# Column sums of squares in a hybrid decoder step: from one float32 product with ones to two float32r products of a larger and a smaller part

## The chip, the cores and the metric

The kernel runs on one core of a Trainium2 chip. The metric is the device time of one execution in microseconds (us); the figure of a kernel is the median of its runs. One execution is also recorded by the hardware profiler, and that record (the page and the trace) is what is read here.

## The reference, cut to what matters

The kernel computes one step of a two-layer decoder for 1024 prompt tokens and 64 sample tokens (1088 columns in all). What the change touches are the sums of squares over the feature axis in three kinds of normalisation:

```
def rmsnorm(x, g):                      # x: (tokens, 1024), before each mixer, each MLP and at the end
    y = xf * rsqrt(mean(xf * xf, axis=-1) + EPS)
    return y * g

def l2norm(x):                          # q and k of each of 4 DeltaNet heads, 128 features
    return xf * rsqrt(sum(xf * xf, axis=-1) + EPS)

o = rmsnorm(o, g_norm) * silu(gate)     # output of each of 8 HGRN2 heads, 128 features
```

Everything else (the projections, the delta rule, latent attention over pages, the HGRN2 recurrence, two squared-ReLU MLPs) is unchanged.

## The kernel before

Activations lie with features on the 128 partitions and tokens along the free axis, in three chunks of 384, 384 and 320 columns. A sum over features is therefore a sum over partitions, and the kernel takes it on TensorE: a product of the squares with a 128 by 128 block of ones leaves the sum in every partition of a PSUM bank.

Dense layers use float32r operands. Each float32 operand is split into a larger part (a ScalarE copy to float32r, line 265) and a smaller part (the float32 value minus that copy, on VectorE, line 266), and three products are added (lines 335 to 337, and 1661 to 1663 for the MLP's second half). The products with ones, on the other hand, have plain float32 operands; the trace shows each as two MATMUL records.

The stages, in time: phase A (0 to about 1040 us: the input projection with its convolution and head work, paged attention of the sample group, prompt attention, the delta rule, the output projection), MLP 0 (to about 1810), the HGRN2 layer (to about 2500), MLP 1 (to about 3262) and the end of the final norm. The three places that the change touches:

- **Norms of x** (`squares`, `split_x`, `inv_rms`, `final_norm`). For each chunk ScalarE squares the eight feature blocks, GpSimd adds blocks 0 to 6 into `ssa` (line 286), the eighth square stays apart in `ssl`, and two float32 products (line 295) add both in one bank. Logarithm, exponential and a Newton step follow (lines 296 to 304) and give `rb`, by which every later evacuation of the projection is multiplied. Four of these norms go through `split_x`; the last, `final_norm`, writes the output at line 1698.
- **Heads of the DeltaNet** (`pairs`). For each of 4 heads, six pieces (k and q, three chunks each): a square (line 699), one float32 product (line 695), logarithm and exponential (689, 690) and a multiplication (691). Behind them stand three blocks of decays: a broadcast load into tile `he` (line 712), sums into `hd` (716), exponentials (717, 718), products of keys (728), and stores to `U_d` and `A_d` (733). `he` and `hd` have one buffer each.
- **Heads of HGRN2** (`core`). For each of 8 heads the squares of the output are gathered in `o2` (line 1883); at the head's end three float32 products (line 1935), logarithms, an exponential, a multiplication and a store. The levels at the head's start write their inputs to tiles of tag `y` (two buffers; lines 1814, 1815, 1818, 1819), which the products at line 1797 read.

Work is written as generators that are woven by weights (`weave`), and a scheduler then orders the instructions of each engine by its own simulated timeline, so each edit can move instructions far from it. Within an engine the order is then fixed. `core(h)` is woven two to one with `proj(h + 1)`, the projection of the next head, whose dense products fill TensorE between the steps of the head.

Of the kernel before, what the change touches and what calls it, by code (L numbers as in the profile page):

```python
# [19 lines left out]
NT = 1088  # L20
# [151 lines left out]
def setup(k, nc, tc, A, O, ctx):  # L172
    k.nc, k.tc, k.A, k.O, k.ctx = nc, tc, A, O, ctx
    k.P = lambda name, bufs=1, **kw: tc.tile_pool(name=name, bufs=bufs, **({} if kw.get("space") == DRAM else {"reuse_waits": "tile"}), **kw)
    k.cp = ctx.enter_context(k.P("consts"))
    k.cst = k.cp.tile([128, NCST], F32, name="cst")
    k.vec = k.cp.tile([128, NVEC], F32, name="vec")
    k.eps = k.cp.tile([128, 2], F32, name="eps")
    k.rb = k.cp.tile([128, NT], F32, name="rb")
    k.dr = ctx.enter_context(k.P("dr", space=DRAM))  # L180
    nc.scalar.preload_act_table_set(EXP_SET)
    nc.gpsimd.memset(k.eps[:, 0:1], EPS)
    nc.gpsimd.memset(k.eps[:, 1:2], EPS * 128)
    C = lambda o, n, p=128: k.cst[0:p, o:o + n]
    k.ident, k.tri, k.maskT = C(C_ID, 128), C(C_TRI, 128), C(C_MT, 128)
    k.tri8, k.mk8, k.ones, k.ones8 = C(C_TRI8, 64, 64), C(C_MK8, 64, 64), C(C_ONE, 128), C(C_ONE8, 64, 64)
    k.V = lambda o: k.vec[:, o:o + 1]
# [76 lines left out]
def split_pair(k, hi, lo, src, eng=None):  # L264
    k.nc.scalar.copy(hi, src)  # L265
    (eng or k.nc.vector).tensor_tensor(lo, src, hi.bitcast(F32), ALU.subtract)  # L266


def rsqrt_from(k, out, ps, scale, bias):

    nc = k.nc
    nc.scalar.activation(out, ps, AF.Ln, bias=bias, scale=scale)
    nc.scalar.activation(out, out, AF.Exp, scale=-0.5)


def squares(k, pool, x, c, n):

    nc = k.nc
    T = lambda tag, name: pool.tile([128, 384], F32, tag=tag, bufs=2, name=name)[:, :n]
    acc = t = T("ssa", f"ssa{c}")  # L280
    for kk in range(8):
        if kk:
            t = T("ssq", f"ssq{c}{kk}") if kk < 7 else T("ssl", f"ssl{c}")
        nc.scalar.activation(t, x[:, kk], AF.Square)  # L284
        if 0 < kk < 7:
            nc.gpsimd.tensor_tensor(acc, acc, t, ALU.add)  # L286
        yield acc, t


def inv_rms(k, pool, sq, c, n, r, ps):  # L290

    nc = k.nc
    p = ps()[:, :n]
    for i in range(2):
        nc.tensor.matmul(p, k.ones, sq[i], start=i == 0, stop=i == 1)
    nc.scalar.activation(r, p, AF.Ln, bias=k.eps[:, 0:1], scale=1.0 / 1024)
    nc.scalar.activation(r, r, AF.Exp, scale=-0.5)
    yield

    v, r2 = (pool.tile([128, 384], F32, tag="nwt", bufs=2, name=f"nwt{c}{i}")[:, :n] for i in range(2))  # L300
    nc.vector.tensor_scalar(v, p, -0.5 / 1024, -0.5 * EPS, ALU.mult, ALU.add)
    nc.scalar.activation(r2, r, AF.Square)
    nc.vector.tensor_tensor(v, v, r2, ALU.mult)
    nc.vector.scalar_tensor_tensor(r, v, 1.5, r, ALU.add, ALU.mult)
    yield


def split_x(k, pool, sqp, x, c, n, g_off, r, ps, xs, lag):

    nc = k.nc  # L310
    hi = pool.tile([128, 8, n], F32R, tag=f"xh{c}", name=f"xh{c}")
    lo = pool.tile([128, 8, n], F32R, tag=f"xl{c}", name=f"xl{c}")
    xs[c] = [(hi[:, kk], lo[:, kk]) for kk in range(8)]
    yield
    s = squares(k, sqp, x, c, n)
    for kk in range(8):
        nc.scalar.mul(hi[:, kk], x[:, kk], k.V(g_off + kk))
        nc.vector.scalar_tensor_tensor(lo[:, kk], x[:, kk], k.V(g_off + kk), hi[:, kk].bitcast(F32),  # L318
                                       ALU.mult, ALU.subtract)
        sq = next(s)  # L320
        yield
    for _ in range(lag):
        yield
    yield from inv_rms(k, sqp, sq, c, n, r, ps)
# [101 lines left out]
def in_proj(k):  # L426
# [247 lines left out]
    def pairs(h, ys, z):  # L674
# [7 lines left out]
        yield  # L682
        items = [(t, t0, n) for t in (kn, q) for t0, n in CH]
        T = lambda i: rp.tile([128, 384], F32, tag="nq", bufs=3, name=f"nq{h}{i}")[:, :items[i][2]]
        r, ps = {}, {}
        for i in range(len(items) + 2):
            if i > 1:
# [4 lines left out]
            if 0 < i <= len(items):  # L692
                n = items[i - 1][2]
                ps[i - 1] = k.mm()[:, :n]
                nc.tensor.matmul(ps[i - 1], k.ones, r[i - 1], start=True, stop=True)
            if i < len(items):
                t, t0, n = items[i]
                r[i] = T(i)
                nc.scalar.activation(r[i], t[:, t0:t0 + n], AF.Square)
            yield  # L700
        nc.sync.dma_start(k.y_d[h, 1], kn)
        egl, egs = k.egl[h], k.egs[h]
# [1001 lines left out]
def hgrn(k, X, before):  # L1704
# [61 lines left out]
    def core(h):  # L1766
# [150 lines left out]
        for c in range(8):  # L1917
# [12 lines left out]
            St = Sn  # L1930
            yield 0.9
        nc.sync.dma_start(O["hgrn_p"][h], St)
        for c, (t0, n) in enumerate(CH):
            p = k.sm()
            nc.tensor.matmul(p[:, :n], k.ones, o2[:, t0:t0 + n], start=True, stop=True)  # L1935
            nc.scalar.activation(o2[:, t0:t0 + n], p[:, :n], AF.Ln, bias=epsd, scale=1.0 / 128)
        nc.scalar.activation(o2, o2, AF.Exp, scale=-0.5)
        nc.vector.tensor_tensor(oz, oz, o2, ALU.mult)
# [57 lines left out]
```

## Time and profile before

| | us |
|---|---|
| median of 3 runs (lowest, highest) | 3300.77 (3298.63, 3304.87) |
| the profiled execution's own time | 3298.84 |
| span of its record | 3297.1 |
| TensorE busy, matmul records | 3163.4 (96%) |
| VectorE / ScalarE / GpSimd busy | 1709.0 / 1107.8 / 543.8 |

Busy time of TensorE is modelled from pipelined records that overlap, so the distance from one record's start to the next is read for a price, and the idle time ahead of an instruction for a wait. A row of the timeline gives start, duration, engine, line, operation, output and inputs, shape and, in brackets, the idle time before it with what ended it; records of one kind that follow one another are merged (x2, x4).

### The profile page before, as it was taken

How to read it: one execution, taken by the hardware profiler on the slowest of the kernel's cores; microseconds unless marked ns; L12 is line 12 of the kernel's file. 1: busy time of each engine (PE TensorE's matmuls, PEld its weight loads, DVE VectorE, ACT ScalarE, POOL GpSimd, SP SyncE). 2: the span in 40 equal slices, each digit the busy share in tenths (PEclk: the TensorE clock that was granted, in tenths of full speed). 3: DMA queues.
4: the chain of work that ended last, by engine and by line, in shares of the span. 5: the costliest groups of instructions: out<-in, count | busy, mean ns of one | idle time of the engine just before them, and what ended most of it. 6: DMA issues, size and time to landing. Idle time of an engine off the chain costs nothing. (4 is left out here: it accounts for less than half of the span.)

```text
span 3297.1 us, 63998 instructions
## 1 busy us (share of the span) xinstructions
PE 3163.4 (96%) x26944; PEld 2928.9 (89%) x26944; DVE 1709.0 (52%) x3102; ACT 1107.8 (34%) x2046; POOL 543.8 (16%) x581
## 2 busy tenths in 40 slices
PE   8999998899989999999999999999899999999997
PEld 7777875687878999999999989889799999999997
DVE  5324443665537445444546555555656444444446
ACT  5334433344415221122123445544535122212212
POOL 3021224112102000000001344443522000000002
PEclk9999999999999999999999999999899999999999
DMA  4666668422132111111112111111322111111111
GB/s 147 199 224 202 218 225 288 149 74 94 57 115 84 45 45 42 43 52 46 33 52 77 56 53 54 53 58 43 131 73 64 33 52 52 45 33 52 46 39 55
DMA packets 140279, 288.70 MB, mean 88 GB/s; under 512 B 16536, under 2 KB 85496, under 8 KB 139992
## 3 DMA queue, kind: packets, MB, share of 16 engines
q1 hardware_dynamic: 118248, 210.60, 19.4%
q10 hardware_dynamic: 12528, 40.45, 3.8%
q0 software_dynamic: 9216, 33.56, 3.1%
q8 instruction: 212, 3.47, 0.4%
q14 instruction: 75, 0.61, 0.1%
HBM read 235.48 MB, written 49.08 MB: 86 GB/s over the span
## 5 line engine op out<-in xcount | busy, mean ns | idle before, releaser
L335 PE MATMUL mm<-xh,wh 128*128 128x384 f32 (+1 forms) x2808 | 936.9, 334 | 12.4 <-ACT wh L265 11.2
L337 PE MATMUL mm<-xh,wl 128*128 128x384 f32 (+1 forms) x2808 | 929.2, 331 | 0.2 <-DVE wl L266 0.2
L336 PE MATMUL mm<-xl,wh 128*128 128x384 f32 (+1 forms) x2808 | 929.0, 331 | 0.0
L1664 DVE TENSOR_TENSOR xr<-xr,sm 128x384 f32<-128x384 f32 (+1 forms) x768 | 404.8, 531 | 430.5 <-PE sm L1663 430.4
L335 PEld LDWEIGHTS mm<-xh,wh 128*128 128x128 f32 x2808 | 531.4, 189 | 23.3 <-ACT wh L265 11.2
L337 PEld LDWEIGHTS mm<-xh,wl 128*128 128x128 f32 x2808 | 531.0, 189 | 9.5 <-issue 6.5
L336 PEld LDWEIGHTS mm<-xl,wh 128*128 128x128 f32 x2808 | 531.0, 189 | 9.1 <-issue 5.1
L1661 PE MATMUL sm<-hh,dh 128*128 128x384 f32 (+1 forms) x1536 | 505.0, 329 | 6.6 <-DVE xr L1664 5.2
L1663 PE MATMUL sm<-hh,dl 128*128 128x384 f32 (+1 forms) x1536 | 503.2, 328 | 0.0
L1662 PE MATMUL sm<-hl,dh 128*128 128x384 f32 (+1 forms) x1536 | 502.5, 327 | 0.0
L286 POOL TENSOR_TENSOR ssa<-ssa,ssq 128x384 f32<-128x384 f32 (+1 forms) x90 | 95.1, 1057 | 1725.0 <-ACT ssq L284 1722.1
L1638 ACT ACTIVATE hraw<-hraw 128x384 f32<-128x384 f32 (+1 forms) x192 | 96.9, 505 | 689.7 <-DVE hraw L1637 689.6
L1661 PEld LDWEIGHTS sm<-hh,dh 128*128 128x128 f32 x1536 | 288.8, 188 | 9.9 <-DVE xr L1664 7.5
L1662 PEld LDWEIGHTS sm<-hl,dh 128*128 128x128 f32 x1536 | 288.6, 188 | 0.6 <-issue 0.2
L1663 PEld LDWEIGHTS sm<-hh,dl 128*128 128x128 f32 x1536 | 288.7, 188 | 0.0
L1637 DVE SCALAR_TENSOR_TENSOR hraw<-mm,rb 128x384 f32<-128x384 f32 (+1 forms) x192 | 102.7, 535 | 184.6 <-PE mm L337 184.5
L265 ACT CAST dh<-dr 128x1024 fp32r<-128x1024 f32 x64 | 66.9, 1048 | 389.6 <-PE sm L1662 381.2
L266 DVE TENSOR_TENSOR hl<-hraw,hh 128x384 fp32r<-128x384 f32 (+1 forms) x192 | 102.3, 533 | 114.8 <-ACT hh L265 114.8
L265 ACT CAST wh<-wr 128x1024 fp32r<-128x1024 f32 x96 | 100.7, 1049 | 137.2 <-PE mm L336 135.3
L266 DVE TENSOR_TENSOR wl<-wr,wh 128x1024 fp32r<-128x1024 f32 x96 | 122.3, 1275 | 37.3 <-ACT wh L265 37.2
L265 ACT CAST hh<-hraw 128x384 fp32r<-128x384 f32 (+1 forms) x192 | 94.9, 494 | 5.1
L928 POOL DMA_INDIRECT lt<-in_lat,ix x64 | 67.0, 1046 | 159.1 <-PE sc L885 66.0
(659 smaller groups left out, 4522.0 us busy)
## 6 DMA issues: line engine op xcount, KB each, us to landing
la<-in_latT SPq DMA_DIRECT2D x256, 144.0 KB, 4.2
wr<-in_w_up SPq DMA_DIRECT2D x64, 512.0 KB, 3.4
dr<-in_w_down ACTq DMA_DIRECT2D x64, 512.0 KB, 4.3
wr<-in_w_in_c SPq DMA_DIRECT2D x32, 512.0 KB, 3.5
win<-in_w_in_ab SPq DMA_DIRECT2D x21, 512.0 KB, 3.9
y_d<-y SPq DMA_DIRECT2D x12, 544.0 KB, 3.1
oC_d<-g SPq DMA_DIRECT2D x8, 544.0 KB, 3.8
q_d<-q SPq DMA_DIRECT2D x16, 256.0 KB, 3.4
```

Of the source, the lines that this page charges most:

```text
L265: k.nc.scalar.copy(hi, src)
L266: (eng or k.nc.vector).tensor_tensor(lo, src, hi.bitcast(F32), ALU.subtract)
L286: nc.gpsimd.tensor_tensor(acc, acc, t, ALU.add)
L335: nc.tensor.matmul(acc, wh[:, kk], xh, start=f, stop=False)
L336: nc.tensor.matmul(acc, wh[:, kk], xl, start=False, stop=False)
L337: nc.tensor.matmul(acc, wl[:, kk], xh, start=False, stop=l)
L1637: nc.vector.scalar_tensor_tensor(raw[:, s], p[:, :n], 0.0, k.rb[:, s], ALU.max, ALU.mult)
L1638: nc.scalar.activation(raw[:, s], raw[:, s], AF.Square)
L1661: nc.tensor.matmul(p[:, :n], wh[:, m], hh[:, s], start=a, stop=False)
L1662: nc.tensor.matmul(p[:, :n], wh[:, m], hl[:, s], start=False, stop=False)
L1663: nc.tensor.matmul(p[:, :n], wl[:, m], hh[:, s], start=False, stop=b)
L1664: nc.vector.tensor_tensor(k.xr[c][:, m], k.xr[c][:, m], p[:, :n], ALU.add)
```

## The change

`ones` gets a float32r copy, `onesr`, made once at the start on GpSimd. `col_sums` adds two products with it, of a larger and a smaller part. The heads' squares (six pieces in each of 4 heads; the whole `o2` in each of 8 heads) are split by `split_pair` first. In `split_x` the two partial sums of x are added on GpSimd, then split, then multiplied; `final_norm` keeps its two float32 products. The split parts of the DeltaNet pieces take the tiles `he` and `hd`; those of `o2` take both buffers of `y`.

```
+    k.onesr = k.cp.tile([128, 128], F32R, name="onesr")
+    nc.gpsimd.memset(k.rb[:, 0:128], 1.0)
+    nc.gpsimd.tensor_copy(k.onesr, k.rb[:, 0:128])
...
+def col_sums(k, p, hl):
+    for i in range(2):
+        k.nc.tensor.matmul(p, k.onesr, hl[i], start=i == 0, stop=i == 1)
...
 def squares(k, pool, x, c, n):
-            t = T("ssq", f"ssq{c}{kk}") if kk < 7 else T("ssl", f"ssl{c}")
+            t = T("ssq", f"ssq{c}{kk}")
...
 def inv_rms(k, pool, sq, c, n, r, ps):
-    for i in range(2):
-        nc.tensor.matmul(p, k.ones, sq[i], start=i == 0, stop=i == 1)
+    if sq[0] is not None:
+        for i in range(2):
+            nc.tensor.matmul(p, k.ones, sq[i], start=i == 0, stop=i == 1)
+    else:
+        col_sums(k, p, sq[1])
...
 def split_x(k, pool, sqp, x, c, n, g_off, r, ps, xs, lag):
+    nc.gpsimd.tensor_tensor(sq[0], sq[0], sq[1], ALU.add)
+    yield
+    hl = [sqp.tile([128, 384], F32R, tag="ss" + i, bufs=1, name=f"ss{i}{c}")[:, :n] for i in "hl"]
+    split_pair(k, *hl, sq[0])
+    sq = None, hl
...
     def pairs(h, ys, z):
+        TR = lambda i, j: rp.tile([128, 512], F32R, tag="hd" if j else "he", bufs=1, name=f"nh{h}{i}{j}")[:, :items[i][2]]
...
-                nc.tensor.matmul(ps[i - 1], k.ones, r[i - 1], start=True, stop=True)
+                col_sums(k, ps[i - 1], hl)
...
                 nc.scalar.activation(r[i], t[:, t0:t0 + n], AF.Square)
+                hl = TR(i, 0), TR(i, 1)
+                split_pair(k, *hl, r[i])
...
     def core(h):
+        hl2 = [hl.tile([128, NT], F32R, tag="y", bufs=2, name=f"oh{h}{i}") for i in range(2)]
+        split_pair(k, *hl2, o2)
         for c, (t0, n) in enumerate(CH):
             p = k.sm()
-            nc.tensor.matmul(p[:, :n], k.ones, o2[:, t0:t0 + n], start=True, stop=True)
+            col_sums(k, p[:, :n], [t[:, t0:t0 + n] for t in hl2])
```

Line numbers of the changed kernel are up to 21 higher: 265 becomes 268, 712 becomes 731, 733 becomes 752, 1664 becomes 1683, 1698 becomes 1717, 1818 becomes 1837, 1883 becomes 1902, 1936 becomes 1957.

What moves, at three places. First ScalarE at the end of one HGRN2 head: `o` is `o2` of the head that ends, `k`, `f`, `x` and `y` belong to the next one. Before:

```order
L1818 COPY y_22809<-k_22760 128x544
L1817 ACTIVATE x_22808<-f_21915 128x544
L1883 ACTIVATE o_22403<-os_22418 128x64
L1883 ACTIVATE o_22403<-sm 128x128
L1875 DMA S_23209<-in_shg 128x1024
```

In the changed kernel, at the same head's end:

```order
L1902 ACTIVATE o_22578<-sm 128x128
L268 CAST oh_22821<-o_22578 128x1088
L1831 COPY x_23059<-f_22090 128x272x2
L1832 ACTIVATE x_23059<-x_23059 128x1088
L1837 COPY y_22991<-k_22942 128x544
L1957 ACTIVATE o_22578<-sm,epsd 128x384 x2
L1957 ACTIVATE o_22578<-sm,epsd 128x320
```

The next head's first `y` (L1818, now L1837) stood ahead of all eight steps of the head that ends; now it stands behind the new split of `o2`.

Second SyncE's queue around the last DeltaNet head. `he<-cum_d` is the load of a decay block, `U_d` and `A_d` the stores of a block's results. The load of the first block stood some fifty rows above these rows. Before:

```order
L360 DMA cq1r<-cq_d 128x2x512
L360 DMA uq1r<-in_w_uq 128x4x256
L733 DMA U_d<-hu_6987 128x512
L733 DMA A_d<-ha_6990 128x512
L712 DMA he_7002<-cum_d 128x4x128
```

In the changed kernel:

```order
L376 DMA cq1r<-cq_d 128x2x512
L376 DMA uq1r<-in_w_uq 128x4x256
L731 DMA he_7087<-cum_d 128x4x128
L752 DMA U_d<-hu_7125 128x512
L752 DMA A_d<-ha_7128 128x512
L731 DMA he_7140<-cum_d 128x4x128
```

The first block's load has come down to stand directly ahead of that block's stores, behind the last of the head's six products.

Third VectorE in the final norm: `xr` are the residual's chunks, L1664 (now L1683) adds a product of the MLP to one, L1698 (now L1717) writes the normalised output of one. Before:

```order
L304 SCALAR_TENSOR_TENSOR rb<-nwt_34642,rb 128x384
L1664 TENSOR_TENSOR xr_26759<-xr_26759,sm 128x320
L1698 SCALAR_TENSOR_TENSOR xr_26758<-xr_26758,vec,rb 128x384 x4
L1664 TENSOR_TENSOR xr_26759<-xr_26759,sm 128x320
L1698 SCALAR_TENSOR_TENSOR xr_26758<-xr_26758,vec,rb 128x384 x4
L301 TENSOR_SCALAR nwt_34703<-sm 128x320
```

In the changed kernel:

```order
L315 SCALAR_TENSOR_TENSOR rb<-nwt_34881,rb 128x384
L1683 TENSOR_TENSOR xr_26976<-xr_26976,sm 128x320
L1717 SCALAR_TENSOR_TENSOR xr_26975<-xr_26975,vec,rb 128x384 x7
L1683 TENSOR_TENSOR xr_26976<-xr_26976,sm 128x320
L1717 SCALAR_TENSOR_TENSOR xr_26975<-xr_26975,vec,rb 128x384
L312 TENSOR_SCALAR nwt_34942<-sm 128x320
```

The last addition to the third chunk stands behind seven output rows of the second instead of four.

## Rows read from the trace of the kernel before

**Rows 1.** Page: busy time of the engines, share of the span, instructions
```profile
PE 3163.4 (96%) x26944; PEld 2928.9 (89%) x26944; DVE 1709.0 (52%) x3102; ACT 1107.8 (34%) x2046; POOL 543.8 (16%) x581
```
**Rows 2.** Windows: HGRN2 stage, end (length, busy PE PEld DVE ACT POOL, clock, DMA)
```profile
1870.00:2345.00 475.00, 452.33 (x5623) 422.31 (x5611) 272.35 (x425) 223.18 (x312) 215.47 (x164) 0.99 0.14 49
3262.00:3297.10 35.10, 18.09 (x85) 14.29 (x83) 25.55 (x46) 11.06 (x23) 11.10 (x12) 0.77 0.36 128
```
**Rows 3.** Timeline of PE: one float32 product among float32r products, 384 and 320 columns
```profile
49.87 0.81 PE L528 MATMUL mm<-cqs,cst 128*128 128x384 f32 x2
50.22 0.63 PE L335 MATMUL mm<-xh,wh 128*128 128x384 f32 x1
50.69 0.34 PE L336 MATMUL mm<-xl,wh 128*128 128x384 f32 x1
51.04 0.34 PE L335 MATMUL mm<-xh,wh 128*128 128x384 f32 x1
...
1946.27 0.70 PE L1935 MATMUL sm<-o,cst 128*128 128x320 f32 x2
1946.96 0.31 PE L335 MATMUL mm<-xh,wh 128*128 128x320 f32 x1
```
**Rows 4.** Source line 695: durations min/median/max in ns, first and last start, shapes
```profile
L695 PE MATMUL mm<-nq,cst x48: 431/485/591, 203.2 to 511.4; 128*128 128x384 f32 x32, 128*128 128x320 f32 x16
```
**Rows 5.** Page, groups: count | busy us, mean ns | idle before, releaser
```profile
L286 POOL TENSOR_TENSOR ssa<-ssa,ssq 128x384 f32<-128x384 f32 (+1 forms) x90 | 95.1, 1057 | 1725.0 <-ACT ssq L284 1722.1
L266 DVE TENSOR_TENSOR hl<-hraw,hh 128x384 fp32r<-128x384 f32 (+1 forms) x192 | 102.3, 533 | 114.8 <-ACT hh L265 114.8
L265 ACT CAST wh<-wr 128x1024 fp32r<-128x1024 f32 x96 | 100.7, 1049 | 137.2 <-PE mm L336 135.3
L266 DVE TENSOR_TENSOR wl<-wr,wh 128x1024 fp32r<-128x1024 f32 x96 | 122.3, 1275 | 37.3 <-ACT wh L265 37.2
```
**Rows 6.** Waits of PE (total, times, longest): products that wait for a split's smaller part
```profile
PE mm L336 <- DVE o2l L266: 2.2, 2, 1.8
PE mm L336 <- DVE o4l L266: 1.9, 2, 1.5
PE mm L336 <- DVE ol L266: 0.5, 1, 0.5
PE mm L336 <- DVE o0l L266: 0.4, 1, 0.4
```
**Rows 7.** Timeline of ACT, POOL and PE: the next head's first tiles, and its first products
```profile
2133.85 0.69 ACT L1818 COPY y<-k 128x544 f32<-128x544 f32 x1
2136.27 2.12 POOL L1819 TENSOR_TENSOR y<-x,q 128x544 f32<-128x544 f32 x1 [5.30 <-ACT x L1817]
2142.01 1.60 POOL L1815 TENSOR_TENSOR y<-x,q 128x544 f32<-128x544 f32 x1
...
2169.78 0.80 PE L1797 MATMUL sm<-q,k 128*32 128x32 f32 x68
```
**Rows 8.** Timeline of SP and DVE: a decay block of the last DeltaNet head
```profile
521.54 0.36 SPq L712 DMA_DIRECT2D he<-cum_d  x1
526.27 1.14 DVE L716 SCALAR_TENSOR_TENSOR hd<-he,nb,cst 128x128 f32<-128x128 f32 x4 [2.04 <-DMA he<-cum_d]
```
**Rows 9.** Timeline of DVE: output rows of the final norm
```profile
3281.53 3.00 DVE L1698 SCALAR_TENSOR_TENSOR xr<-xr,vec,rb 128x384 f32<-128x384 f32 x4
3284.85 2.19 DVE L1698 SCALAR_TENSOR_TENSOR xr<-xr,vec,rb 128x384 f32<-128x384 f32 x4
```
**Rows 10.** Timeline of PE: waits ahead of the first norm's products
```profile
20.30 0.91 PE L295 MATMUL mm<-ssa,cst 128*128 128x384 f32 x2 [1.42 <-POOL ssa L286]
32.04 0.91 PE L295 MATMUL mm<-ssa,cst 128*128 128x384 f32 x2 [1.85 <-POOL ssa L286]
```
**Rows 11.** Timeline of DVE: one multiplication while GpSimd ran subtractions, and one without
```profile
494.98 0.56 DVE L691 TENSOR_TENSOR y<-y,nq 128x384 f32<-128x384 f32 x1 [1.80 <-ACT nq L690]
495.75 4.76 DVE L691 TENSOR_TENSOR y<-y,nq 128x384 f32<-128x384 f32 x1 [0.22 <-ACT nq L690]
```

## The prediction

> **What bounds the kernel now.** The page's first section comes first: matmul records fill 96% of the span on TensorE, the next engine stands at 52% [rows 1]. Busy time of overlapping records proves little, so I look next at the windows: in the HGRN2 stage TensorE is without a record for 475 - 452.3 = 22.7 us, one twentieth [rows 2]. Time taken from TensorE there is therefore time taken from the span, as long as no new wait appears in its place. The end is another thing: in its last 35.1 us VectorE is busy for 25.6 and TensorE for 18.1 [rows 2]. There the order on VectorE decides.
>
> **What the products cost.** From the timeline of TensorE, by starts: from a float32 product of 384 columns at 49.87 to 50.69 is 0.82 us, with one float32r product in it (start 50.22); a float32r product takes (51.04 - 50.69) / 2 = 0.175 us [rows 3]. So the float32 product holds the engine for 0.645 us, two float32r products for 0.35. With 320 columns: 1946.96 - 1946.27 = 0.69, less one float32r product (0.175 x 320/384 = 0.146), is 0.544 us; two float32r products are 0.292 [rows 3].
> - DeltaNet heads: 48 records, two for each product, 32 of 384 columns and 16 of 320 [rows 4], so 16 and 8 products. Saved: 16 x 0.295 + 8 x 0.252 = 6.7 us.
> - HGRN2 heads: 8 heads with the same three chunks, so again 16 and 8 products of the same kind, 6.7 us.
> - Norms of x: four of the five change, each with chunks of 384, 384, 320. Two float32 products become two float32r products: 4 x (2 x (1.29 - 0.35) + (1.088 - 0.292)) = 10.7 us.
>
> Together **-24.1 us** on TensorE, all in stages that it fills.
>
> **What is added elsewhere.** ScalarE gets 36 copies to float32r of a chunk and 8 of 1088 columns (1.05 x 1088/1024 = 1.11 us), VectorE as many subtractions (0.53 us, and 1.275 x 1088/1024 = 1.35), GpSimd 12 additions of 1.06 [rows 5]. As engine time this is free, since those engines are busy 52%, 34% and 16% [rows 1]; if TensorE did not cover it, it would be 8 x 2.46 us for the HGRN2 heads alone. It costs by being late:
>
> *Splits before a product.* 44 new splits stand directly ahead of a product (12 norms, 24 pieces, 8 heads). The trace has 44 splits of that kind in the output projections (`ol`, `wol`, `o0l` to `o4l`), and TensorE waited 2.2 + 1.9 + 0.5 + 0.4 = 5.0 us for their smaller parts [rows 6]. The bounds are 0, if the scheduler puts enough dense products between the copy and the product, and 44 x 1.1 = 48, if every split were as exposed as the two of `o2l` (2.2 / 2). The new splits are of the size of `ol` and `wol`, 34 of those 44, of which the rows show one wait of 0.5. I take the mean over all 44: **+5.0 us**.
>
> *The last DeltaNet head.* `he` and `hd` are taken by the split pieces, so the load for the first decay block now waits for the sixth product. For the first three heads the dense products behind it cover that; for the last they are finished, and the prompt preparation's stores queue on SyncE behind the block's stores. From the load's issue to the end of the four sums is 526.27 + 1.14 - 521.54 = 5.9 us [rows 8], with exponentials some 7. Bounds 0 and +7. I take **+2**, nearer the lower: the sample group's attention, which needs nothing of this head, is still being worked off on TensorE then (by the order of the work; no row prices that cover).
>
> *HGRN2 heads.* The split of `o2` takes both `y` buffers, so the next head's first two `y` tiles wait until the column sums are read. Now they are done early: the second ends at 2142.01 + 1.60 = 2143.6, and its products follow those of 2169.78 [rows 7]. Afterwards the path between two heads has the split (1.11 + 1.35) and then y0 (2.12) and y1 (two of 1.60): 7.8 us more. The dense products of the next projection cover it if there are enough of them; the head is woven with 288, about 47 us of TensorE. I cost it at nothing beyond the splits above; without that cover it is a rival below. What is late next is the multiplication of level two on GpSimd.
>
> *Front.* TensorE waited 1.42 and 1.85 us for GpSimd's sums [rows 10]. Each now becomes an addition (1.06), a copy and a subtraction longer, but other dense products are ordered ahead. Bounds -3.3 (both waits filled) and +2.1 (one chain of 1.06 + 0.5 + 0.53 exposed); taken as 0. Making `onesr` on GpSimd, idle then, costs nothing; the first chunk's sums would feel it otherwise.
>
> *End.* `final_norm` keeps its products, but three more output rows go before the last addition: 3 x 2.19/4 = 1.6 us, or 3 x 3.00/4 = 2.3 [rows 9]. Against that the last addition of 384 columns comes ahead of the first eight output rows, which frees a bank earlier. Bounds -1 and +2.3; taken **+1**.
>
> Sum: -24.1 + 5.0 + 2 + 1 = -16.1 us. The profiled execution took 3298.84 us, which gives 3282.7; it lies 1.9 below the median of the runs, so on the scale of the median **3285 us**. A difference of 0.2%, 6.6 us, is about what a measurement can tell from none.
>
> **A rule that speaks against it.** One multiplication of 384 columns took 0.56 us alone and 4.76 while GpSimd ran subtractions [rows 11]. The Trainium skill, "SBUF — State Buffer", section "SBUF: two separate sides", says that a VectorE operation with two SBUF inputs and a GpSimd operation lock each other out of a shared port pair for a whole instruction. The added subtractions are of that kind; by that rule each would be held for up to one GpSimd operation, and the row agrees. This is rival B.
>
> **The rivals.**
> - A, everything is gained: the waits of rows 10 are filled and no split is waited for. -24.1 - 3.3 = -27 us, 3273. For it: the scheduler has put dense products between the larger and the smaller part's product. Against: rows 6. Chance 0.12.
> - B, the splits eat most of it: the subtraction is held behind a GpSimd operation of 1.06 us [rows 5] in half of the 44 splits, and half of that reaches TensorE: 22 x 1.06 x 0.5 = 11.7 more than forecast, 3297. For: row 11; in HGRN2 GpSimd is busy 215 of 475 us [rows 2]. Against: in the norms it has ended its own sums by then. Chance 0.14.
> - C, slower: the path from head to head bounds HGRN2, because `y` is not free. There are seven head boundaries with 7.8 us each. From 16.1 / 7 = 2.3 us exposed at each the gain is gone; with half of the 7.8 exposed at all seven it is 27 more than forecast, 3312. For: 22.7 us in which TensorE already stands, part of it for `y`. Against: y0 and y1 were ready 26 us early [rows 7], so the path had slack. Chance 0.10.
> - D, the change doesn't do what it says: a product of `onesr` runs at the float32 rate, so nothing is saved and 48 products of some 0.6 us come on top, 3301 + 29 + 8 = 3338. Against: weights made by the same copy run at 0.175 us [rows 3]. Chance 0.02.
>
> **How the numbers follow.** The forecast, a gain of 7 to 24 us, has 0.62. Faster by over 0.2%: 0.62 + 0.12 and 0.02 of B, 0.76. Within 0.2%: the rest of B with a little of C, 0.13. Slower: most of C and D, 0.11. The range runs from A, 3273, to C's beginning with two boundaries wholly exposed, 3285 + 15.6, 3300.
>
> **What would show it.** The records of lines 695 and 1935 gone, 120 of `col_sums` in their place at 0.175 us from start to start; line 295's down to 12 for the final norm. Waits of TensorE for `nh`, `ssl` or `oh` near 5 us in total. In HGRN2 a window shorter by about 6 us for the same dense work; if it is not shorter, and products with `y` wait on GpSimd after each boundary, C is right. Between 511 and 560 us the first use of the next stage at most 2 us late. At the end the last addition about 1 us later against the start of the final norm. The prediction is wrong if the waits on TensorE grow by more than 17 us, or by none.

## The result, and the profile after

| | before | after |
|---|---|---|
| median (lowest, highest), us | 3302.07 (3298.63, 3305.09) | 3335.39 (3324.58, 3341.0) |
| ratio of after to before, 95% interval | | 1.0102, 1.0084 to 1.012 |
| the profiled execution's own time, its span | 3298.84, 3297.1 | 3330.14, 3328.4 |

The change is 33 us slower where 16 us faster was forecast; the time lies 35 us above the range. The page of the changed kernel gives the busy times that answer to [rows 1]:

```profile
PE 3157.2 (95%) x26920; PEld 2940.0 (88%) x26920; DVE 1769.9 (53%) x3146; ACT 1139.3 (34%) x2096; POOL 557.1 (17%) x595
```

TensorE has 6 us less to do than before, VectorE 61 us more. Where the time went is seen by stage. From the first evacuation of HGRN2's first projection (line 1762, now 1781) to the last head's last multiplication (1938, now 1959) it was 626.9 us and is 669.2. The windows of that stage, before (columns as in [rows 2]):

```profile
1820.90:2447.80 626.90, 590.41 (x6859) 548.56 (x6858) 353.12 (x554) 287.62 (x405) 259.43 (x191) 0.97 0.18 60
```

After, and below it one period of the seventh head, from the first GpSimd tile of one head to that of the next:

```profile
1816.00:2485.20 669.20, 606.76 (x6929) 572.38 (x6928) 387.85 (x565) 304.72 (x421) 257.13 (x191) 0.94 0.16 57
...
2343.36:2401.73 58.37, 41.62 (x646) 37.13 (x644) 38.57 (x60) 36.60 (x52) 31.92 (x24) 0.82 0.45 158
```

Of the 42.3 us, 25.9 are time in which TensorE has no record (62.4 against 36.5). Of the other 16.4 some 12.3 are work that has moved into the stage: the output projection of the first five heads (products with `woh` and `wol`) has 328 records in it instead of 250, busy for 65.6 us instead of 53.3. Behind the stage 84 records and 12.6 us are fewer; the windows of what is left of the span, before and after:

```profile
2447.80:3297.10 849.30, 828.00 (x4960) 820.73 (x4958) 442.61 (x757) 209.68 (x364) 37.86 (x36) 0.99 0.15 50
2485.20:3328.40 843.20, 815.40 (x4876) 808.68 (x4874) 444.18 (x754) 209.22 (x367) 41.46 (x39) 0.99 0.16 50
```

So some 30 of the 42.3 us are lost, and the 6.1 us that are won back behind the stage are less than the work that left it. The stage's other records, 8 fewer than before, take 548.9 us instead of 545.2, at a granted clock of 0.94 instead of 0.97. In the seventh head's period TensorE is without a record for 16.8 of 58.4 us at a clock of 0.82; the products of the next projection that fill the other heads are used up there before the head's end.

The place where it starts is the boundary of two heads. ScalarE before, from the third head's last square (line 1883, into `o`) to the next head's copy of its last value block (`vt<-sm`, line 1775), which needs the next head's first transposes; the timeline, columns as in [rows 7]:

```profile
2088.06 0.27 ACT L1883 ACTIVATE o<-sm 128x128 f32<-128x128 f32 x1
...
2090.22 0.58 ACT L1936 ACTIVATE o<-sm,epsd 128x384 f32<-128x384 f32 x1
2091.80 0.58 ACT L1936 ACTIVATE o<-sm,epsd 128x384 f32<-128x384 f32 x1 [1.00 <-PE sm L1935]
2093.55 0.53 ACT L1936 ACTIVATE o<-sm,epsd 128x320 f32<-128x320 f32 x1 [1.17 <-PE sm L1935]
...
2095.13 0.24 ACT L1775 COPY vt<-sm 64x128 f32<-64x128 f32 x1
```

The same boundary after:

```profile
2092.03 0.26 ACT L1902 ACTIVATE o<-sm 128x128 f32<-128x128 f32 x1
...
2093.19 1.08 ACT L268 CAST oh<-o 128x1088 fp32r<-128x1088 f32 x1
2098.09 0.70 ACT L1837 COPY y<-k 128x544 f32<-128x544 f32 x1 [3.82 <-PE sm L274]
2099.14 1.47 ACT L1957 ACTIVATE o<-sm,epsd 128x384 f32<-128x384 f32 x3 [0.35 <-PE sm L274]
...
2101.98 1.13 ACT L1958 ACTIVATE o<-o 128x1088 f32<-128x1088 f32 x1
2103.99 0.26 ACT L1794 COPY vt<-sm 64x128 f32<-64x128 f32 x1
```

From the last square to that copy it was 7.1 us and is 12.0. Over the seven boundaries: 7.6, 6.5, 7.1, 8.0, 7.4, 7.7 and 3.0 us before, 12.8, 12.1, 12.0, 13.1, 12.5, 8.2 and 12.0 after; the sum grows by 35 us. Before, the first logarithm came 2.2 us after the last square, because the first two sums need only earlier columns of `o2`; now all three stand behind one split of the whole row, 7.1 us. And the first `y` tile, made 25 us ahead of a head's last square before (2136.27 in [rows 7], the square at 2161.40), now begins 6 us behind it:

```profile
2098.14 1.62 POOL L1838 TENSOR_TENSOR y<-x,q 128x544 f32<-128x544 f32 x1 [32.35 <-PE sm L274]
...
2104.33 1.08 POOL L1896 TENSOR_TENSOR vx<-vt,cst 64x512 f32<-64x512 f32 x1 [0.90 <-ACT vt L1794]
2105.37 1.34 POOL L1833 TENSOR_TENSOR y<-x,k 128x544 f32<-128x544 f32 x1
2106.68 1.34 POOL L1834 TENSOR_TENSOR y<-x,q 128x544 f32<-128x544 f32 x1
```

TensorE's waits in the stage, longest sums first (us in total, times, longest); before, TensorE's waits for `y` were 7.9 and 3.2 us, and no projection waited for `g`:

```profile
PE mm L351 <- DVE g L1781: 15.7, 3, 7.2
PE sm L1856 <- POOL y L1834: 15.1, 6, 5.4
...
PE sm L1816 <- POOL y L1834: 4.8, 2, 3.3
...
PE sm L274 <- ACT oh L268: 2.0, 1, 2.0
```

The three waits for `g` are a projection that cannot run further ahead: by the program a `g` tile stays taken until the late head's result is stored. So the loss shows at TensorE mostly in places other than the sums themselves, which wait for 2.0 us here and 0.6 for the smaller part.

### The profile page after: what moved, and what is told of

Read it like the earlier page. It is cut to its first block, busy times and chain, and to the rows that moved or that the text cites. A ratio compares the mean times of both kernels' runs of the same rounds, so it can differ in the third digit from the quotient of the medians.

```text
span 3328.4 us, 64124 instructions
## 1 busy us (share of the span) xinstructions
PE 3157.2 (95%) x26920; PEld 2940.0 (88%) x26920; DVE 1769.9 (53%) x3146; ACT 1139.3 (34%) x2096; POOL 557.1 (17%) x595
## 4 chain that ended last, share of the span: by engine, by line
PE 69%; DVE 6%; DMA 2%; ACT 2%; POOL 2%; issue 2%; SPq 0%; DVEq 0%; ACTq 0%; POOLq 0%
PE mm L353 12%; PE mm L351 12%; PE mm L352 12%; PE sm L1680 7%; PE sm L1682 7%; PE sm L1681 7%; PE po L1452 1%; PE tr L1460 1%; DVE xl L329 1%; POOL y L1834 1%; DVE x L1830 1%; DVE f L1839 1%; PE mm L1077 1%; POOL y L1833 1%; PE sc L1423 1%
## 5 line engine op out<-in xcount | busy, mean ns | idle before, releaser
L1683 DVE TENSOR_TENSOR xr<-xr,sm 128x384 f32<-128x384 f32 (+1 forms) x768 | 404.6, 531 | 431.1 <-PE sm L1682 430.9
L1839 DVE TENSOR_TENSOR f<-f 128x512 f32<-128x512 f32 (+1 forms) x56 | 79.0, 1411 | 42.2 <-ACT x L1836 22.9
```

Of the source, the lines that this page charges most:

```text
L1683: nc.vector.tensor_tensor(k.xr[c][:, m], k.xr[c][:, m], p[:, :n], ALU.add)
L1839: nc.vector.tensor_tensor(up(f), up(f), tot, ALU.add)
```

## The experiments

Ratios are to the kernel before, run beside each; 0.001 is 3.3 us. First the HGRN2 heads and what in their edit costs, then the norms, then the pairs.

**HGRN2 put back.**

```
-        split_pair(k, *hl2, o2)
...
-            col_sums(k, p[:, :n], [t[:, t0:t0 + n] for t in hl2])
+            nc.tensor.matmul(p[:, :n], k.ones, o2[:, t0:t0 + n], start=True, stop=True)
```

> The changed kernel with its HGRN2 heads put back to float32 products of o2 with ones (norms of x and DeltaNet pairs keep the float32r products). Theory H, the loss is made by the edit of the HGRN2 heads alone: the rest keeps the 6.8 us by which the changed kernel was ahead at the start of HGRN2 and the 6 to 7 us that it won back after it, so about 13 us below the kernel before, 3289, and HGRN2 as long as before (588 us from the first product to the last multiplication, not 631). Rival G, the loss is not the edit's own but the order that the scheduler makes when the earlier stages end earlier: HGRN2 stays over 610 us and the time over 3310.

1.0001 (0.9989 to 1.0014), HGRN2 626.6 us. The loss is the heads' edit, as H had it. But the remaining edits, which should gain 13 us, gain nothing; that is a second miss, taken up below. The 6 to 7 us "won back" among those 13 were no gain to begin with: they are less than the output projection's work that had moved into HGRN2.

**The HGRN2 heads alone**, the same edit on the kernel before:

```
+        hl2 = [hl.tile([128, NT], F32R, tag="y", bufs=2, name=f"oh{h}{i}") for i in range(2)]
+        split_pair(k, *hl2, o2)
...
-            nc.tensor.matmul(p[:, :n], k.ones, o2[:, t0:t0 + n], start=True, stop=True)
+            col_sums(k, p[:, :n], [t[:, t0:t0 + n] for t in hl2])
```

> The kernel before with only the HGRN2 heads changed (split of the whole o2 into both buffers of y, float32r sums). If the loss is this edit's alone: the changed kernel's ratio less that of norms and pairs, 1.0102 - 1.0001, so 1.010, 3335. If the scheduler's order in the other edits had a part in it: 1.007 or less.

1.0112 (1.0096 to 1.0129): +37 us, by this edit alone.

**Pieces in dead tiles**, so that `y` stays free:

```
+        hl2 = [hl.tile([128, NT], F32R, tag="qg", bufs=1, name=f"oh{h}0"),
+               hl.tile([128, 9, 128], F32R, tag="kt", bufs=1, name=f"oh{h}1").rearrange("p c t -> p (c t)")[:, 0:NT]]
```

> The changed kernel, but the two pieces of o2 lie in the tiles of qg and kt, which are dead at the end of a head, instead of both buffers of y. The head's end is as late as in the changed kernel, but the next head's first two y tiles can be made early. Theory Y (the loss is the hold of y): the loss goes, HGRN2 is some 6 us shorter than before, 3283 to 3290. Theory S (the loss is the split itself, 1.1 us on ScalarE and 1.3 on VectorE between the last square and the sums, on a path from head to head that also runs through the sums' PSUM banks): 7 boundaries of 2.4 us stay, 3299 or more; if the hold adds nothing at all, 3335.

1.0054 (1.0036 to 1.0073). The hold of `y` is worth 0.0048, 16 us; the rest stays, as S said, and more than its 2.4 us a boundary: the boundaries sum to 71 us, against 47 before.

**One buffer of `y` held** (larger part in `qg`, smaller part in `y`):

```
+        hl2 = [hl.tile([128, NT], F32R, tag="qg", bufs=1, name=f"oh{h}0"),
+               hl.tile([128, NT], F32R, tag="y", bufs=2, name=f"oh{h}1")]
```

> The changed kernel with the larger part of o2 in the dead tile of qg and only the smaller part in a buffer of y. Both buffers held: 1.0102 of before; none held: 1.0054. If what counts is that no y tile can be made ahead beyond the first: the first tile is early, the second late, half, 1.008. If the slowed VectorE additions beside GpSimd are what the hold costs (1.41 us each instead of 0.93 for 56 of them): the mean of those additions says so, near 1.41 with 1.010 or near 0.93 with 1.005.

1.0078 (1.0063 to 1.0092), half of the hold. VectorE's additions of `f`, before, after and here (instructions by line in HGRN2: busy us, mean ns, then idle time before them):

```profile
L1820 DVE TENSOR_TENSOR f<-f 128x512 f32<-128x512 f32 (+1 forms) x56 | 52.1, 931 | 42.5 <-ACT x L1817 42.4
```

```profile
L1839 DVE TENSOR_TENSOR f<-f 128x512 f32<-128x512 f32 (+1 forms) x56 | 79.0, 1411 | 42.2 <-ACT x L1836 22.9 <-ACT x L1831 18.9
```

```profile
L1839 DVE TENSOR_TENSOR f<-f 128x512 f32<-128x512 f32 (+1 forms) x56 | 55.8, 997 | 41.9 <-ACT x L1836 26.3 <-ACT x L1831 15.2
```

With one buffer held the additions are nearly as short as before and half of the loss is there; so the late `y` tile costs by itself, and the slowed additions aren't needed for it. What share they have in the other half no run tells.

**The split in chunks**, each right ahead of its sums, pieces in `y`:

```
-        split_pair(k, *hl2, o2)
         for c, (t0, n) in enumerate(CH):
             p = k.sm()
+            split_pair(k, *[t[:, t0:t0 + n] for t in hl2], o2[:, t0:t0 + n])
```

> The changed kernel, but o2 of an HGRN2 head is split in its three chunks of 384, 384 and 320 columns, each split right ahead of its own sums, instead of in one piece of 1088; the pieces still lie in both buffers of y. Theory P (most of the loss is that one split of the whole row makes the first sum wait for the last square and for both 1088-column steps, and the next head's first transposes wait for a PSUM bank behind those sums): the time from a head's last square to the next head's copy of its last value block falls from 12 us to 8 or 9 (before: 7 to 8), HGRN2 is within 10 us of before, 3300 to 3310. Theory Y (the hold of y costs most): 12 us there stay about as they are, or y stays late, 3320 or more.

1.0077 (1.0062 to 1.0093). P was right on the boundary (5.7 us in the mean, less than before) and wrong on the time: the chunks give 0.0025, 8 us. The boundaries sum to 40 us, 43 less than in the changed kernel, but most of that is lost behind them. From the value copy to the last level's first GpSimd multiplication the later seven heads take 162 us, 148 before and 160 in the changed kernel; from there to a head's first square the eight heads take 206 us, 188 before and 184 in the changed kernel.

**Chunks, and `y` free**, the two edits together:

```
+        hl2 = [hl.tile([128, NT], F32R, tag="qg", bufs=1, name=f"oh{h}0"),
+               hl.tile([128, 9, 128], F32R, tag="kt", bufs=1, name=f"oh{h}1").rearrange("p c t -> p (c t)")[:, 0:NT]]
         for c, (t0, n) in enumerate(CH):
             p = k.sm()
+            split_pair(k, *[t[:, t0:t0 + n] for t in hl2], o2[:, t0:t0 + n])
```

> As the kernel with chunkwise splits, but with the pieces in the dead tiles of qg and kt, so that y is free for the next head. If hold and lump add up (the hold was worth 3335 - 3320 = 16 us, the lump the rest of the 20 us that stayed), this is the best of the four arrangements, 3293 to 3300. If the split's own latency stays on the path (0.5 us on ScalarE and 0.5 on VectorE for a chunk, and the dense products that the scheduler puts ahead of it: 48 of them stand between the last recurrence product and the next head's transposes in this program, 30 with y, 35 before), 3310 or more.

1.0029 (1.0016 to 1.0042). The hold of `y` and the split of the whole row in one lump add up: 0.0054 - 0.0029 is again 0.0025, and 0.0077 - 0.0029 again 0.0048; each difference is uncertain by some 0.002, so that they meet to the last digit is luck. But 9.6 us stay, as the second branch of the expectation had it, with 6.7 us of TensorE saved: the boundaries sum to 62 us, 15 more than before, since a chunk's copy and subtraction still stand between the last square and the last sum. With `y` free the account closes: time lost and the 6.7 us together are 16 us for 15 at the boundaries here, and 25 us (18 + 6.7) for 24 with the whole row split.

**Two banks instead of three:**

```
             St = Sn
+            if c == 3:
+                p = k.sm()
+                nc.tensor.matmul(p[:, :64], k.ones, o2[:, SEQ:NT], start=True, stop=True)
+                nc.scalar.activation(o2[:, SEQ:NT], p[:, :64], AF.Ln, bias=epsd, scale=1.0 / 128)
...
-        for c, (t0, n) in enumerate(CH):
+        for t0, n in ((0, 512), (512, 512)):
```

> The changed kernel with the sums of a head taken in two pieces of 512 columns at its end (split piece by piece, pieces in y) and the 64 sample columns summed as float32 after the fourth of its eight steps. The head's end then takes two of the three small PSUM banks instead of all three. Theory B (the next head's start waits for a bank that a logarithm must free): the next head's value copy comes one logarithm earlier, 6 to 7 us after the last square, and the time is below the chunkwise version's by 5 us or more, near or below 3300. If the bank isn't what is waited for: equal to the chunkwise version, within 3 us.

1.0075 (1.0058 to 1.0092), the same as in chunks. The value copy comes 5.4 us after the last square in the mean, a little earlier, but the levels take 188 us. The bank is not what sets the time while `y` is held.

**A delay and nothing else**, on the kernel before:

```
         nc.sync.dma_start(O["hgrn_p"][h], St)
+        for _ in range(2):
+            nc.scalar.copy(o2, o2)
```

> The kernel before, with o2 copied onto itself twice on ScalarE (2 x 1.1 us) between the last square of an HGRN2 head and its column sums; no split, no float32r, y untouched. Theory S (the head's end lies on the path from head to head and dense products don't cover it): 7 to 8 heads of 2.2 us, 15 to 18 us slower, 3317 to 3320. Theory Y (only the y tiles matter, the end of a head is covered as the prediction assumed): 3302 to 3305.

1.0104 (1.0084 to 1.0123): the whole loss of the change, with no float32r and `y` untouched. Two copies of 1.12 us cost 34 us over eight heads, 4.3 each; the boundaries sum to 78 us, 30 more than before. That the time is that of the whole change is chance, since here nothing is held and nothing saved on TensorE. ScalarE at the third boundary (the copies at line 1934):

```profile
2106.26 0.26 ACT L1883 ACTIVATE o<-sm 128x128 f32<-128x128 f32 x1
2106.55 2.24 ACT L1934 COPY o<-o 128x1088 f32<-128x1088 f32 x2
...
2113.12 1.71 ACT L1938 ACTIVATE o<-sm,epsd 128x384 f32<-128x384 f32 x3 [2.02 <-PE sm L1937]
...
2117.36 0.26 ACT L1775 COPY vt<-sm 64x128 f32<-64x128 f32 x1 [1.39 <-PE sm L1773]
```

The copies take the whole row, so they also join the three chunks: from the last square to the first logarithm it is 6.9 us instead of 2.2. That the path from head to head sets HGRN2's time, with TensorE's work unchanged, is shown by this run.

**The four norms alone**, on the kernel before, edited as in the change:

```
+    nc.gpsimd.tensor_tensor(sq[0], sq[0], sq[1], ALU.add)
...
+    split_pair(k, *hl, sq[0])
+    sq = None, hl
```

> The kernel before with only the four norms of x changed (partial sums added, split, float32r products); DeltaNet and HGRN2 heads keep float32 products. By the prediction's terms: 10.7 us saved on TensorE less some 2 us for 12 splits, 3293. If splits and additions in front of a norm's product are exposed (12 of about 2 us), no gain: 3302. The difference to the kernel with norms and pairs is what the pairs are worth (predicted 6.7 saved, 2.7 for splits, 2 for the last head, so 2 us).

1.0011 (1.0 to 1.0022), not 3293 us but 3.6 us slower. The stretch from the first GpSimd sum of the norm ahead of HGRN2 to the first evacuation behind it, before:

```profile
1789.50:1820.90 31.40, 28.11 (x155) 25.33 (x154) 31.40 (x60) 23.41 (x52) 21.83 (x23) 1.00 0.39 140
```

and with the norms changed:

```profile
1785.70:1822.00 36.30, 29.14 (x149) 27.10 (x148) 36.27 (x64) 24.35 (x55) 24.95 (x26) 0.91 0.35 124
```

The third busy time is VectorE's: all of the stretch, in both. TensorE fills 28.1 of 31.4 us, so it is VectorE that has no room here.

**The norm ahead of HGRN2 put back** to float32, pairs and the other three norms changed:

```
+    if g_off != V_MIX + 8:
         nc.gpsimd.tensor_tensor(sq[0], sq[0], sq[1], ALU.add)
...
         split_pair(k, *hl, sq[0])
         sq = None, hl
```

> Norms of x and DeltaNet pairs changed, HGRN2 heads with float32 products, and also the norm ahead of HGRN2 put back to float32 products of both partial sums. Theory V (VectorE, not TensorE, bounds that norm: from its first GpSimd sum to the first evacuation of the next projection VectorE is busy for all of the time, 31.4 us before, 36.3 with three more subtractions and multiplications slowed beside GpSimd): the stretch is 31.4 us again, and the time falls by up to 4.9 us against the kernel that differs only there (ratio 1.0001 to before), to 0.999 of before. Rival T (TensorE bounds it, as the prediction had it): the float32 products come back, +2.6 us, 1.001 of before.

0.9981 (0.9968 to 0.9993); the stretch is 32.0 us. V holds: giving TensorE its float32 products back made the kernel faster than with all four norms changed (1.0001), by 0.002, about as much as the two intervals together can tell.

**VectorE's work in that norm raised**, on the kernel before:

```
+        if g_off == V_MIX + 8 and kk % 2:
+            nc.vector.scalar_tensor_tensor(lo[:, kk], x[:, kk], k.V(g_off + kk), hi[:, kk].bitcast(F32),
+                                           ALU.mult, ALU.subtract)
```

> The kernel before, with four VectorE operations of each chunk of the norm ahead of HGRN2 done twice (the smaller part of x, 12 more operations of 0.54 us alone, up to 1.2 beside GpSimd); nothing on TensorE changes. Theory V: that stretch grows from 31.4 by 6.5 to 13 us, and the time by as much, 1.002 to 1.004 of before. Rival T (TensorE sets that norm's time): no change, within 0.001.

1.0014 (1.0003 to 1.0024), 4.6 us, between the rival's 0.001 and V's 0.002, with an interval that covers both. The stretch grows by 8.7 us, as V had it, and about half of that shows in the time:

```profile
1787.00:1827.10 40.10, 32.55 (x169) 29.10 (x168) 40.03 (x75) 23.66 (x53) 22.48 (x23) 0.96 0.32 112
```

**Only the larger part in the norms:**

```
-    split_pair(k, *hl, sq[0])
+    nc.scalar.copy(hl[0], sq[0])
...
-    for i in range(2):
-        k.nc.tensor.matmul(p, k.onesr, hl[i], start=i == 0, stop=i == 1)
+    k.nc.tensor.matmul(p, k.onesr, hl[0], start=True, stop=True)
```

> Only the four norms of x changed, and of the two parts only the larger one is made and multiplied: the smaller part of the sums of squares is left out. VectorE then has no more to do than before; GpSimd keeps the added sum and ScalarE the copy. Theory V: the stretch from the first GpSimd sum of the norm ahead of HGRN2 to the first evacuation after it falls from 36.3 to 32 us and the one ahead of MLP 0 from 47.4 to 45; against the version with both parts (1.0011 of before) 5 to 9 us faster, 0.9985. If it is the longer chain of GpSimd, ScalarE and product that costs: 36 us stay, 1.001. If TensorE bound the norms: 12.7 us below before, 0.996.

0.9973 (0.9963 to 0.9984), 12.5 us below the run with both parts, more than V's 5 to 9. Each chunk also loses one product on TensorE, some 2 us in all, and the time lies between V's 0.9985 and the 0.996 of a bound on TensorE, so by itself it decides nothing between them. The stretch is 33.7 us, shorter by 2.6 but not the 32 that V expected, and VectorE still fills it:

```profile
1783.30:1817.00 33.70, 26.80 (x147) 25.35 (x146) 33.70 (x59) 24.52 (x54) 24.88 (x26) 0.95 0.38 133
```

**The subtraction moved to GpSimd**, pairs and all four norms changed:

```
-    split_pair(k, *hl, sq[0])
+    split_pair(k, *hl, sq[0], nc.gpsimd)
```

> Pairs and all four norms changed, HGRN2 heads with float32 products, and the smaller part of the norms' sums subtracted on GpSimd instead of VectorE (complete result). Theory V (VectorE's load in the norms is what cost): as pairs alone (0.9972 of before) and some of the 12 us that leaving the subtraction out gave: 0.995 to 0.998. If the longer chain through GpSimd or the port that both share takes it back: as with the subtraction on VectorE, 1.000.

1.0011 (0.9997 to 1.0024): nothing won, the rival. VectorE is rid of three subtractions in the stretch and yet busy for 36.8 of 37.8 us, with GpSimd at 28.4 instead of 21.8:

```profile
1794.60:1832.40 37.80, 29.55 (x151) 26.92 (x150) 36.82 (x63) 25.05 (x56) 28.43 (x29) 0.91 0.35 122
```

What is left on VectorE takes longer: the subtraction that makes a smaller part of x has a median of 958 ns in that stretch, 894 with the norm's subtraction on VectorE and 687 before.

**The pairs alone**, on the kernel before:

```
-                nc.tensor.matmul(ps[i - 1], k.ones, r[i - 1], start=True, stop=True)
+                col_sums(k, ps[i - 1], hl)
...
+                hl = TR(i, 0), TR(i, 1)
+                split_pair(k, *hl, r[i])
```

> The kernel before with only the six pieces of each DeltaNet head split and summed by float32r products. The prediction's terms: 6.7 us saved on TensorE, 24 of 44 splits (2.7) and 2 for the last head given back, so 2 us faster, 3300. By the difference of two runs (norms and pairs 1.0001, norms alone 1.0011 of before) 3 us faster. Wrong if it is slower, or faster by more than 8 us.

0.9972 (0.996 to 0.9984): 9 us faster, the best complete version of all, and faster than both kernels. By the 8 us set as its limit the expectation of 2 us was wrong. TensorE waits for a smaller part once, 2.8 us; the last product of keys (line 728) starts at 529.7 us, 530.4 before, so the last head is not late.

**Which norm takes the pairs' gain away:** the pairs with the first norm, the first norm alone, and the pairs with the norms of the two MLPs.

```
+    if g_off == V_MIX:
...
+    if g_off in (V_MLP, V_MLP + 8):
```

> Pairs and only the first of the four norms of x (at the start of the program) changed; the norms ahead of the MLPs and of HGRN2 and the HGRN2 heads keep float32 products. Theory V (the norms ahead of MLP 0 and of HGRN2 are bound by VectorE, which is busy for 93% and 100% of them, so float32r there gains nothing): not worse than the version with three norms changed (0.9981 of before), 0.997 to 0.999. Rival T (each changed norm gains 2.6 us on TensorE): 5 us slower than that version, 0.9996.

> The kernel before with only the first norm of x (at the start of the program) changed. If the first norm is what gives the pairs' gain away: 5 to 8 us slower, 1.0015 to 1.0025 of before, and the first DeltaNet rsqrt begins 3 to 4 us later than before (204.8 us). The prediction's term for it: 2.6 saved, nothing lost, 3300, 0.9992; then the loss lies in the MLPs' norms.

> Pairs and the two norms ahead of the MLPs changed; the first norm, the norm ahead of HGRN2 and the HGRN2 heads keep float32 products. If the first norm is the one that costs: as the pairs alone or a little better, 0.996 to 0.9975 of before. If the MLPs' norms give it away (the one ahead of MLP 0 has VectorE busy for 93% of it): 0.999 or more.

0.9996 (0.9985 to 1.0008), 1.001 (1.0 to 1.0019) and 0.9988 (0.9978 to 0.9998). Norms added to the pairs cost: the first about 8 us with them and 3.3 alone, those of the MLPs some 5, which the two intervals don't set clear of nothing. In the run of the first norm alone the first DeltaNet rsqrt starts at 208.3 us instead of 204.8, as expected. TensorE's waits from 14 to 60 us there, where before there were 3.3 us for GpSimd's sums:

```profile
PE mm L354 <- DVE wl L269: 3.5, 1, 3.5
PE mm L352 <- ACT wh L268: 1.7, 1, 1.7
PE mm L352 <- DVE cq L505: 0.6, 1, 0.6
```

The waits of [rows 10] are filled, as forecast, and 5.8 us of others stand in their place. That the pairs with the first norm and both MLPs' norms gave 0.9981 doesn't fit additive parts of this size; which of the norms costs what stays open below some 5 us.

## Why the prediction was wrong

The parts, each measured alone, add up to the whole: heads +37, norms +3.6, pairs -9.2, sum +31; measured together +33. Predicted were, with each part's share of the 5.0 us for splits, -5.8, -8.3 (with the end) and -2.

**The step that failed first: "The dense products of the next projection cover it if there are enough of them ... I cost it at nothing beyond the splits above".** There weren't enough. [rows 7] were read as slack, because two `y` tiles lay ready 26 us early. But early as they were, they were not on the path; the path ran from the last square through sums and logarithm to the next head's transposes, 7 us at each boundary. Nor do early tiles keep the boundary short (with `y` held and chunks it is 5.7 us); they shorten the levels behind it. The order of the program on TensorE shows the price: between a head's last recurrence product and the next head's last value transpose stood 35, 28, 33, 35, 31, 35 and 0 products of the next projection, in the changed program 65, 58, 66, 67, 59, 44 and 0; 162 more, of 0.175 us at most, are up to 28 us of dense work spent at boundaries. (At the last boundary 12 products of the output projection stand in the changed program.) Between the first and the last recurrence product of the seventh head none is left, where 18 of the output projection stood before. Dense work in a woven stage is a supply, and a longer path is paid from it until it is gone. The 0 was already there in the program before. This is not all of the loss: with chunks and `y` held the boundaries take 190 such products, fewer than before (197), and 25 us are lost all the same, behind the boundaries.

**Rival C was the right mechanism, too small and incomplete.** It priced 7.8 us at each boundary and took half of it as a case. Against the forecast the heads are off by 37 + 5.8 = 43 us, 6.1 at each of seven boundaries. Some 16 us are the hold that C names; 8 are the joining of three chunks into one split, which no term had; the rest, some 19, fits the split's own latency on the path, which the forecast priced with the mean wait of all 44 splits, 0.11 us, and C with 2.46 of its 7.8 us.

**"Time taken from TensorE there is therefore time taken from the span"** was the reading behind it, under the condition that no new wait appears. [rows 2] show TensorE without a record for one twentieth of HGRN2, and 2.2 us of ScalarE's time at a head's end cost 4.3 us all the same.

**The second step that failed: "As engine time this is free, since those engines are busy 52%, 34% and 16%".** These are shares of the span. The norm ahead of HGRN2 has VectorE busy for 31.40 of 31.40 us, the one ahead of MLP 0 for 41.84 of 44.90. The norms' 10.7 us on TensorE bought nothing. That VectorE fills that stretch in six kernels shows the bound there; the times alone, each near the edge of its interval, would not, and for the other norms it is argued. The Trainium skill, "Perfetto Trace Analysis", section "Optimization Strategy", says that the most contended engine can change from one regime of a kernel to another; the trace agrees, VectorE 100% in that stretch and 52% over the span.

**Rival B** had the right engines and the wrong victim. The splits are hardly held: TensorE's waits for `nh`, `ssh`, `ssl`, `oh` come to about 14 us in the changed kernel, where 5 were forecast, and over half of it is put down to ScalarE's copy, not to the subtraction. What is held are other VectorE operations. An addition of `f` took 0.72 us alone and 4.17 beside the GpSimd rows of 2104.33 to 2106.68 shown above:

```profile
2092.16 0.72 DVE L1839 TENSOR_TENSOR f<-f 128x544 f32<-128x544 f32 x1
...
2104.43 4.17 DVE L1839 TENSOR_TENSOR f<-f 128x544 f32<-128x544 f32 x1
```

The Trainium skill, "SBUF — State Buffer", section "SBUF: two separate sides", has it that a VectorE operation with two SBUF inputs and a GpSimd operation that reads SBUF exclude each other from a port pair for a whole instruction; that row agrees, and the run whose subtraction went to GpSimd is in line with it. But the prediction's "held for up to one GpSimd operation" was too little: the addition ends 0.6 us behind the last of three GpSimd operations in a row, and the 4.76 us of [rows 11] likewise span three subtractions in a row, 496.37 to 500.08.

**The other terms.** The prices were right. D fell: three float32r sums of 384, 384 and 320 columns take 2099.27 - 2098.77 = 0.50 us, and 0.175 x 1088 / 384 is 0.496:

```profile
2098.77 0.66 PE L274 MATMUL sm<-oh,onesr 128*128 128x384 f32 x3
2099.27 0.31 PE L352 MATMUL mm<-xl,wh 128*128 128x320 f32 x1
```

The end: from the final norm's first GpSimd sum to the start of the last addition it is 29.9 us before and 30.8 after, the 1 us that was taken. The pairs: forecast -2, measured -9 (-13 to -5). The 2 us for the last head were not paid, and the whole saving of 6.7 us lies within the interval. So the saving on TensorE seems to have reached the time just where the forecast expected least. The front: taken as 0, measured +3.3 alone (0 to 6.3).

## What to carry to other kernels

Read an engine's busy share in the stretch that an edit touches, not over the span: an engine at half load on the page can be the bound there, and a subtraction put on it can then cost more than the product that it saves. In a stage where a chain is woven with filler work, a filler engine that is 95% busy proves nothing; put a small delay at the chain's end and see whether the time follows. A split of a whole row in front of sums that were taken chunk by chunk, and buffers borrowed from the next step's first tiles, each cost time, even where ScalarE and VectorE are busy for only about half of the stage (288 and 353 of 627 us before).

## What the runs showed of the hardware that was not expected

The granted clock of TensorE fell in a stage that it fills for over nine tenths: 0.94 in the mean of HGRN2 instead of 0.97 (between its two levels, 1.2 and 2.4 GHz), and 0.82 in the period where the next projection's products had run out. What that cost is small against the stalls themselves: 25.9 us more without a record, and 3.7 us more in the records of the same work, its cheaper sums included. One VectorE addition stood beside three GpSimd operations in a row and took 4.17 us instead of 0.72. And relieving VectorE by giving a subtraction to GpSimd did not relieve it: 36.8 us of VectorE's time in the norm with three subtractions fewer, 36.3 with them, 31.4 before either.
